# Differential attention: the second half of head 1's Q is projected during head 1 in place of head 0

## The chip, the cores and the metric

The kernel runs on one core of a Trainium2 chip. The metric is the device time of one execution in microseconds. The kernel before was timed in three runs.

## What is computed

The program is a decoder trunk of two layers over 1024 tokens of width 1024. In each layer a retention group and a differential attention group read the same normed input, their outputs are projected together, and a SwiGLU block follows. The change is in the differential attention, whose four heads each have two score matrices:

```python
dq.reshape(B, S, DIFF_HEADS, 2, DIFF_HEAD_DIM)
...
for i in range(S // Q_BLOCK):
    q0 = i * Q_BLOCK
    kend = q0 + Q_BLOCK
    ...
    s = jnp.einsum('bqhjd,bkhjd->bhjqk', qb, kb).astype(jnp.float32) * scale
    s = s - slopes[None, :, None, None, None] * dist
    s = jnp.where(dist >= 0, s, -jnp.inf)
    p = jax.nn.softmax(s, axis=-1)
    a = p[:, :, 0] - lam * p[:, :, 1]
    outs.append(jnp.einsum('bhqk,bkhe->bqhe', a.astype(vb.dtype), vb))
```

There are 8 query blocks of 128 tokens. Block i needs Q of its own 128 tokens and K and V of all tokens up to its end, so blocks 0 to 3 need only the first half (512 tokens) of Q, K and V.

## The kernel before

**Products in three parts.** An operand is kept as a high part rounded to the matmul's input type and the low part that is left, and each fp32 product is made as three matmuls (high·high, high·low, low·high; lines 288 to 290 by `mm3`). `fm_half` projects one half of the tokens for one head's Q or K: 8 blocks of the width by 3 matmuls of 128x512, so 24 matmuls into one accumulation bank `ps_mm`. `stack` then turns that bank into the two tiles that the scores read (one for each score matrix j): an ACT copy of 64x512 (line 522) and a DVE subtraction of the same size (line 523), twice. `stacks` does this for the halves that it is given, and `qk_head` for both halves of K and then both halves of Q of a head.

**One attention block** (`att_block`). The scores of block i for j=1 are made in chunks of at most 512 keys, each chunk two matmuls (lines 574 and 575) into one score bank `ps_s`. DVE adds the bias and takes the maximum of a chunk (line 577), which frees the bank; ACT takes the exponential (581) and scales by the row sum (657); then the same for j=0; the two are combined on DVE (line 666). The combined block is transposed on PE in the next block's turn (line 600), copied in two parts by ACT and DVE (605, 606), and every second block an output product follows (lines 619 to 622 into `ps_o`), with ACT's copy and square (624, 629), a split of the square in two parts (ACT line 370, DVE line 372), and the norm of each 512 tokens, whose two ones-matmuls on PE (line 380) read that split.

**Banks.** There are two score banks `ps_s`, three `ps_mm`, two `ps_t` and one `ps_o`. A chunk of scores may begin once DVE has taken the chunk that stood two before it.

**The order of the work.** PE's order is the order in which the program is written, and a scheduler sets that of ACT, DVE, POOL and SP; what stands under `high_priority` is brought forward there. `weave` (line 342) mixes an attention stretch ("main") with projections for later ("fill"): after each yield of the main stretch, which names a cost, it draws groups of three fill matmuls until the fill's share of its total has caught up with the main's share of its total. `PART0` is 72, the cost of blocks 0 to 3, and `PART1` is 92, that of blocks 4 to 7. Fill drawn within a head makes K and Q of the next head: beside blocks 4 to 7 of head 0 it is `qk_head` for head 1 (96 matmuls over 92), beside all eight blocks of head 1 it is `qk_head` for head 2 (96 over 164). Where the fill runs over, the rest is written behind the stretch.

**Transfers.** A weight is loaded by SP as one DMA of 512 KB, cast by ACT (line 280) and its low part made by POOL (line 281). `att_swap` issues four SP copies of 128 KB for a half of a head: they place K of one score matrix on the partitions on which the other's Q stands (tile `kb`).

Both layers run the same order of instructions in the attention.

Of the kernel before, what the change touches and what calls it, by code (L numbers as in the profile page):

```python
# [38 lines left out]
PART0 = HEAD + 2 * 6 + 4 * sum(LAG)  # L39
PART1 = 2 * 22 + 4 * sum(LAG)  # L40
# [107 lines left out]
class Trunk:  # L148
# [538 lines left out]
    def attention(self, l, us, w_first, norm1):  # L687
        wk, wq, wdv = w_first
        nc = self.nc
        v, qk, outs = {}, self.qk_tiles(), []  # L690
        kq = lambda hf: self.chain(self.stacks(wk, us, (hf,), qk[1], 1.0), self.stacks(wq, us, (hf,), qk[0], 0.125))
        first = [self.chain(kq(hf), self.values(wdv, us, hf, v)) for hf in range(NH)]
        if l == 0:
            for ps, st, scale in zip(self.first_ps, (qk[1], qk[0]), (1.0, 0.125)):
                f = self.tmp()
                nc.vector.tensor_tensor(out=f, in0=ps, in1=self.first_y, op=ALU.mult)
                self.stack(f, st, slice(0, HT), scale)
            self.weave(norm1, 40, self.values(wdv, us, 0, v), 48)
            self.late_consts()
        else:  # L700
            self.weave(norm1, 96, first[0], 96)
        self.prev, self.norms, self.outs = None, [], []
        for h in range(4):
            o = self.big("mx")
            outs.append(o)
            A = self.att_open(h, qk, v, o)
            nqk = self.qk_tiles() if h < 3 else None
            self.att_swap(A, 0)
            if h:
                self.att_swap(A, 1)  # L710
            if h == 0:
                self.weave(self.att_part(l, A, 0, 4), PART0, first[1], 96)
                self.att_swap(A, 1)
            elif h == 2:
                self.weave(self.att_part(l, A, 0, 4), PART0, self.values(wdv, us, 1, v), 48)
            if h == 3:
                rq = [self.big("ka") for _ in range(2)]
                rk = [self.big("a4") for _ in range(2)]
                fill = self.chain(self.ret_proj(us, rq[0], 1.0), self.ret_proj(us, rq[1], 1.0),
                                  self.ret_proj(us, rk[0], 0.125), self.ret_proj(us, rk[1], 0.125))  # L720
            else:
                fill = self.qk_head(us, nqk)
            if h % 2:
                self.weave(self.att_part(l, A, 0, 8), PART0 + PART1, fill, 96 if h == 1 else 192)
            else:
                self.weave(self.att_part(l, A, 4, 8), PART1, fill, 96)
            if h < 3:
                qk = nqk
            if h == 1:
                wdv = [self.weight(), self.weight()]  # L730
                v = {}
                self.weave(self.att_close(l), 48, self.values(wdv, us, 0, v), 48)
        return outs, rq, rk
# [556 lines left out]
```

## Time and profile before

| | us |
|---|---|
| median of three runs | 2291.52 (2290.36 to 2292.31) |
| the profiled execution | 2289.39 |
| its span in the profile | 2287.6 |
| TensorE matmul busy (share of the span) | 2251.1 (98%) |
| VectorE busy | 1404.7 (61%) |
| ScalarE busy | 1009.1 (44%) |
| GpSimd busy | 731.7 (32%) |

PE is TensorE's matmuls and PEld its weight loads, DVE is VectorE, ACT is ScalarE, POOL is GpSimd and SP is the engine that issues the DMAs. A timeline row has an instruction's start, its length, the engine, the line and the operation with output and inputs, and in square brackets the idle time before it and who ended it. Matmuls overlap: a 128x512 matmul has a length of 0.39 us on its row, and the next one starts about 0.23 us after it, so stretches of PE are reckoned from start to start. The mean granted clock was 0.996 of full speed.

### The profile page before, as it was taken

The page shows a single profiled execution, that of the slowest core. Times are in us where ns is not written, and L with a number is a line of the kernel's source. Part 1 is how long each engine was busy: PE and PEld are TensorE (multiplying, and loading weights), DVE is VectorE, ACT ScalarE, POOL GpSimd, SP SyncE. Part 2 cuts the span into 40 slices and gives each one's busy share as a digit, 9 for nine tenths or more (in the row PEclk, how much of TensorE's full clock was granted, in tenths as well). Part 3 has the DMA queues.
Part 4 walks back from the last instruction along what each step waited for, and adds up shares of the span by engine and source line. Part 5 has one row for each costly group of instructions (what it writes and reads, how often), then busy time and mean ns, then how long its engine had stood idle before and what let it go on. Part 6 is the DMA issues. An engine that isn't in the chain of part 4 may idle for free.

```text
span 2287.6 us, 30632 instructions
## 1 busy us (share of the span) xinstructions
PE 2251.1 (98%) x11328; PEld 1895.3 (83%) x11328; DVE 1404.7 (61%) x2596; ACT 1009.1 (44%) x1905; POOL 731.7 (32%) x588
## 2 busy tenths in 40 slices
PE   7999999999999999999999999999999999999998
PEld 5888898787888888888888888988878888888887
DVE  8777612989534333995567774059884434359856
ACT  5666523445333333543256665234453333344332
POOL 3111212120455555335121112211215445544350
PEclk9999999999999999999999999999999999999999
DMA  4212121112433333652232222112123232346422
GB/s 164 79 47 65 44 95 38 55 57 63 137 106 103 105 106 90 230 186 96 72 99 56 56 65 88 52 37 74 49 95 120 93 115 93 110 148 202 157 65 74
DMA packets 74215, 216.58 MB, mean 95 GB/s; under 512 B 8017, under 2 KB 10065, under 8 KB 74065
## 3 DMA queue, kind: packets, MB, share of 16 engines
q1 hardware_dynamic: 74064, 214.62, 29.1%
q8 instruction: 89, 1.46, 0.3%
q14 instruction: 62, 0.50, 0.1%
HBM read 162.16 MB, written 44.04 MB: 90 GB/s over the span
## 4 chain that ended last, share of the span: by engine, by line
PE 84%; DVE 11%; ACT 2%; issue 1%; DMA 1%; POOL 0%; SPq 0%; DVEq 0%; ACTq 0%; POOLq 0%
PE ps_mm L264 8%; PE ps_mm L265 8%; PE ps_mm L266 8%; PE ps_mm L289 7%; PE ps_mm L288 7%; PE ps_mm L290 7%; PE ps_s L265 4%; PE ps_s L264 4%; PE ps_s L266 4%; PE ps_mm L323 3%; PE ps_mm L324 3%; PE ps_mm L325 3%; PE ps_t L265 2%; PE ps_t L264 2%; PE ps_t L266 2%
## 5 line engine op out<-in xcount | busy, mean ns | idle before, releaser
L241 POOL TENSOR_TENSOR w<-wr,w 128x512 fp32r<-128x512 f32 x262 | 368.2, 1419 | 442.9 <-ACT w L240 425.6
L281 POOL TENSOR_TENSOR w<-wr,w 128x512 fp32r<-128x512 f32 x140 | 186.2, 1337 | 577.3 <-ACT w L280 520.7
L288 PE MATMUL ps_mm<-u,w 128*128 128x512 f32 (+1 forms) x735 | 296.1, 403 | 0.0
L289 PE MATMUL ps_mm<-u,w 128*128 128x512 f32 (+1 forms) x735 | 287.2, 391 | 2.4 <-DVE u L450 2.4
L290 PE MATMUL ps_mm<-u,w 128*128 128x512 f32 (+1 forms) x735 | 286.5, 390 | 0.0
L240 ACT CAST w<-wr 128x512 fp32r<-128x512 f32 x312 | 187.2, 619 | 136.5 <-DVE wr L911 77.5
L264 PE MATMUL ps_mm<-u,w 128*128 128x512 f32 x432 | 168.5, 390 | 0.0
L266 PE MATMUL ps_mm<-u,w 128*128 128x512 f32 x432 | 168.1, 389 | 0.0
L265 PE MATMUL ps_mm<-u,w 128*128 128x512 f32 x432 | 168.1, 389 | 0.0
L290 PEld LDWEIGHTS ps_mm<-u,w 128*128 128x128 f32 x735 | 138.1, 188 | 30.1
L289 PEld LDWEIGHTS ps_mm<-u,w 128*128 128x128 f32 x735 | 138.6, 189 | 26.0 <-DVE u L450 3.1
L288 PEld LDWEIGHTS ps_mm<-u,w 128*128 128x128 f32 x735 | 138.3, 188 | 23.7
L960 ACT COPY t<-ps_mm 128x512 f32<-128x512 f32 x76 | 44.7, 588 | 240.3 <-PE ps_mm L266 240.3
L280 ACT CAST w<-wr 128x512 fp32r<-128x512 f32 x140 | 85.7, 619 | 128.6 <-PE ps_t L289 39.6
L325 PE MATMUL ps_mm<-w,u 128*128 128x256 f32 x448 | 127.2, 284 | 0.8 <-DVE u L450 0.8
L323 PE MATMUL ps_mm<-w,u 128*128 128x256 f32 x448 | 128.0, 286 | 0.0
L324 PE MATMUL ps_mm<-w,u 128*128 128x256 f32 x448 | 126.9, 283 | 0.0
L241 POOL TENSOR_TENSOR w<-t,w 128x512 fp32r<-128x512 f32 x48 | 65.1, 1357 | 191.9 <-ACT w L240 191.9
L577 DVE CUSTOM_DVE_ANT_0 sp<-ps_s,wr 128x512 f32<-128x512 f32 (+2 forms) x192 | 102.9, 552 | 32.3 <-PE ps_s L575 31.3
L581 ACT ACTIVATE sp<-sp,m 128x256 f32<-128x256 f32 (+7 forms) x128 | 99.2, 775 | 50.2 <-DVE m L580 49.4
L869 DVE TENSOR_TENSOR a<-a,ps_mm 128x512 f32<-128x512 f32 (+1 forms) x148 | 98.6, 667 | 27.6 <-PE ps_mm L266 14.5
L909 DVE TENSOR_TENSOR t<-wr,wr 128x512 f32<-128x512 f32 x46 | 32.8, 712 | 119.2 <-DMA wr<-wts 118.5
(386 smaller groups left out, 5919.7 us busy)
## 6 DMA issues: line engine op xcount, KB each, us to landing
wr<-wts SPq DMA_DIRECT2D x190, 512.0 KB, 3.7
mx<-s_fast SPq DMA_DIRECT2D x56, 512.0 KB, 4.9
s_fast<-mx SPq DMA_DIRECT2D x48, 512.0 KB, 4.8
kb<-ka SPq DMA_DIRECT2D x64, 128.0 KB, 2.3
s_rest<-mx SPq DMA_DIRECT2D x12, 512.0 KB, 2.9
kb<-wts SPq DMA_DIRECT2D x12, 512.0 KB, 5.4
mx<-s_rest SPq DMA_DIRECT2D x12, 512.0 KB, 3.3
a<-xT SPq DMA_DIRECT2D x16, 256.0 KB, 5.4
```

Of the source, the lines that this page charges most:

```text
L240: nc.scalar.copy(h, src)
L241: (eng or nc.gpsimd).tensor_tensor(out=o, in0=src, in1=h.bitcast(F32), op=ALU.subtract)
L264: mm(ps, lhsT=wh[:, c], rhs=bh, start=first and i == 0, stop=False, skip_group_check=True)
L265: mm(ps, lhsT=wh[:, c], rhs=bl, start=False, stop=False, skip_group_check=True)
L266: mm(ps, lhsT=wl[:, c], rhs=bh, start=False, stop=i == 3, skip_group_check=True)
L281: nc.gpsimd.tensor_tensor(out=o, in0=raw[:, cols], in1=h.bitcast(F32), op=ALU.subtract)
L288: mm(out, lhsT=lh, rhs=rh, start=first, stop=False)
L289: mm(out, lhsT=lh, rhs=rl, start=False, stop=False)
L290: mm(out, lhsT=ll, rhs=rh, start=False, stop=last)
L323: mm(o, lhsT=uh, rhs=wh, start=k == 0, stop=False)
L324: mm(o, lhsT=uh, rhs=wl, start=False, stop=False)
L325: mm(o, lhsT=ul, rhs=wh, start=False, stop=k == KT - 1)
```

## The change

In head 0's second stretch the fill now makes K of head 1 for the first half of the tokens, Q for the first half, and K for the second half: 72 matmuls over `PART1`. Head 1's weights for K and Q are both requested ahead of it. In head 1 the fill begins with Q of head 1 for the second half of the tokens, and `qk_head` of head 2 follows: 120 matmuls over 164. Heads 2 and 3 stay as they are. In each of the two layers this moves 24 matmuls of 128x512 and one `stack`.

```diff
@@ -718,12 +718,18 @@
+            elif h == 0:
+                wk1, wq1 = self.weight(), self.weight()
+                fill = self.chain(self.stacks(wk1, us, (0,), nqk[1], 1.0), self.stacks(wq1, us, (0,), nqk[0], 0.125),
+                                  self.stacks(wk1, us, (1,), nqk[1], 1.0))
             else:
                 fill = self.qk_head(us, nqk)
+                if h == 1:
+                    fill = self.chain(self.stacks(wq1, us, (1,), qk[0], 0.125), fill)
             if h % 2:
-                self.weave(self.att_part(l, A, 0, 8), PART0 + PART1, fill, 96 if h == 1 else 192)
+                self.weave(self.att_part(l, A, 0, 8), PART0 + PART1, fill, 120 if h == 1 else 192)
             else:
-                self.weave(self.att_part(l, A, 4, 8), PART1, fill, 96)
+                self.weave(self.att_part(l, A, 4, 8), PART1, fill, 96 if h else 72)
```

**PE, the scores of block 4 of head 1 in layer 0.** The first two `ps_s` are the two chunks of block 4 for j=1, the last one is the first chunk for j=0, and `ps_mm` is the bank of a fill product. Before:

```order
L574 MATMUL ps_s_1376<-ka_472,a_106_470 128x512
L575 MATMUL ps_s_1376<-kb_1123,a_106_470 128x512
L574 MATMUL ps_s_1380<-ka_472,a_106_470 128x256
L575 MATMUL ps_s_1380<-kb_1123,a_106_470 128x256
L288 MATMUL ps_mm_1295<-u_350,w_1144 128x512
L289 MATMUL ps_mm_1295<-u_351,w_1144 128x512
L290 MATMUL ps_mm_1295<-u_350,w_1145 128x512
L574 MATMUL ps_s_1393<-ka_471,a_105_469 128x512
```

The changed kernel, the same scores:

```order
L574 MATMUL ps_s_1361<-ka_472,a_106_470 128x512
L575 MATMUL ps_s_1361<-kb_1094,a_106_470 128x512
L574 MATMUL ps_s_1365<-ka_472,a_106_470 128x256
L575 MATMUL ps_s_1365<-kb_1094,a_106_470 128x256
L288 MATMUL ps_mm_1339<-u_350,w_1227 128x512
L289 MATMUL ps_mm_1339<-u_351,w_1227 128x512
L290 MATMUL ps_mm_1339<-u_350,w_1228 128x512
L288 MATMUL ps_mm_1339<-u_350,w_1227 128x512
L289 MATMUL ps_mm_1339<-u_351,w_1227 128x512
L290 MATMUL ps_mm_1339<-u_350,w_1228 128x512
L574 MATMUL ps_s_1381<-ka_471,a_105_469 128x512
```

Two groups of three fill matmuls stand between the two score matrices where one stood. From head 0's last output product to the second of these chunks there were 30 fill matmuls and are now 33, and from it to the second j=1 chunk of block 5 there were 9 and are now 15. The other 15 of the 24 that are moved are drawn in the rest of head 1 and ahead of that product.

**ACT, behind head 0's last output product (`ps_o_1209` before, `ps_o_1176` now).** `ps_mm_1109` is the bank of head 1's Q for the second half of the tokens. Before:

```order
L624 COPY mx_464<-ps_o_1209 128x256
L629 ACTIVATE t_247_1235<-mx_464 128x512
L370 CAST t_248_1237<-t_247_1235 128x512
L581 ACTIVATE sp_1199,z_1200<-sp_1199,m_1246 128x256
L605 CAST a_252_1257<-ps_t_1261 128x128
L522 ACTIVATE ka_1128<-ps_mm_1148 64x512
```

The changed kernel:

```order
L624 COPY mx_464<-ps_o_1176 128x256
L629 ACTIVATE t_241_1202<-mx_464 128x512
L280 CAST w_1680<-wr_1674 128x512
L522 ACTIVATE a_105_469<-ps_mm_1109 64x512
L370 CAST t_242_1204<-t_241_1202 128x512
L605 CAST a_252_1239<-ps_t_1243 128x128
L581 ACTIVATE sp_1163,z_1164<-sp_1163,m_1210 128x256
L522 ACTIVATE a_106_470<-ps_mm_1109 64x512
```

A weight's cast (line 280) and the first copy of the moved `stack` (line 522) have come between the square (line 629) and its split (line 370); the second copy stands four rows on.

**DVE, around the scores of blocks 3 and 4 of head 1.** Line 577 takes a chunk of scores and frees its bank. Before:

```order
L577 ISA sp_1321,m_1344<-ps_s_1345,wr_1124 128x512
L577 ISA m_1344 128x1
L666 SCALAR_TENSOR_TENSOR sp_1269<-sp_1269,z_1270 128x384
L388 SCALAR_TENSOR_TENSOR t_261_1284<-t_260_1282,t_261_1284 128x512
L582 RECIPROCAL z_1322<-z_1322 128x1
L580 TENSOR_REDUCE m_1344<-m_1344 128x1
L636 SCALAR_TENSOR_TENSOR mx_464<-mx_464,c_dg,t_261_1284 128x512
L606 TENSOR_TENSOR a_274_1359<-ps_t_1362,a_273_1358 128x3x128
L656 TENSOR_TENSOR z_1322<-z_1322,c_nlam 128x1
L582 RECIPROCAL z_1322<-z_1322 128x1
L577 ISA sp_1373,m_1375<-ps_s_1376,wr_1124 128x512
```

The changed kernel:

```order
L666 SCALAR_TENSOR_TENSOR sp_1251<-sp_1251,z_1252 128x384
L388 SCALAR_TENSOR_TENSOR t_261_1266<-t_260_1264,t_261_1266 128x512
L582 RECIPROCAL z_1302<-z_1302 128x1
L523 SCALAR_TENSOR_TENSOR ka_1099<-ps_mm_1235,ka_1099 64x512
L636 SCALAR_TENSOR_TENSOR mx_464<-mx_464,c_dg,t_261_1266 128x512
L606 TENSOR_TENSOR a_274_1344<-ps_t_1347,a_273_1343 128x3x128
L523 SCALAR_TENSOR_TENSOR ka_1100<-ps_mm_1235,ka_1100 64x512
L656 TENSOR_TENSOR z_1302<-z_1302,c_nlam 128x1
L577 ISA sp_1301,m_1324<-ps_s_1325,wr_1095 128x512
L577 ISA m_1324 128x1
L577 ISA sp_1358,m_1360<-ps_s_1361,wr_1095 128x512
L577 ISA m_1360 128x1
```

The L577 that takes block 3's j=0 scores (`ps_s_1345`, now `ps_s_1325`) stood ahead of line 666 and now stands behind it, behind both L523 of the next `stack`, and directly ahead of the two chunks of block 4.

## Rows read from the trace of the kernel before

**Rows 1.** The page, busy time of each engine (share of the span) and instructions.

```profile
PE 2251.1 (98%) x11328; PEld 1895.3 (83%) x11328; DVE 1404.7 (61%) x2596; ACT 1009.1 (44%) x1905; POOL 731.7 (32%) x588
```

**Rows 2.** Windows: length, busy PE, PEld, DVE, ACT, POOL; clock, DMA share, GB/s.

```profile
73.50:110.30 36.80, 36.80 (x194) 31.35 (x192) 28.06 (x78) 24.96 (x46) 7.36 (x10) 1.00 0.27 72
110.30:154.80 44.50, 42.56 (x237) 35.10 (x235) 38.43 (x121) 32.07 (x70) 5.99 (x11) 1.00 0.17 44
1236.10:1280.60 44.50, 42.59 (x237) 35.09 (x236) 38.38 (x121) 32.07 (x70) 6.03 (x12) 1.00 0.17 43
```

**Rows 3.** Timeline of PE, end of head 0 and head 1's blocks 3 to 5.

```profile
104.07 0.39 PE L288 MATMUL ps_mm<-u,w 128*128 128x512 f32 x1
...
106.80 0.93 PE L600 MATMUL ps_t<-c_ident,sp 128*128 128x128 f32 x7
...
116.25 0.40 PE L288 MATMUL ps_mm<-u,w 128*128 128x512 f32 x1
...
126.28 0.39 PE L290 MATMUL ps_mm<-u,w 128*128 128x512 f32 x1
127.40 0.52 PE L600 MATMUL ps_t<-c_ident,sp 128*128 128x128 f32 x3 [0.72 <-DVE sp L666]
...
128.91 0.28 PE L574 MATMUL ps_s<-ka,a 128*128 128x256 f32 x1
...
129.62 0.39 PE L290 MATMUL ps_mm<-u,w 128*128 128x512 f32 x1
129.99 0.50 PE L574 MATMUL ps_s<-ka,a 128*128 128x512 f32 x1
...
132.87 0.39 PE L575 MATMUL ps_s<-kb,a 128*128 128x512 f32 x1
134.18 0.35 PE L574 MATMUL ps_s<-ka,a 128*128 128x256 f32 x1 [0.92 <-DVE z L656]
```

**Rows 4.** Timeline of ACT, behind head 0's last output product and at a stack.

```profile
117.19 0.63 ACT L629 ACTIVATE t<-mx 128x512 f32<-128x512 f32 x1
117.86 0.62 ACT L370 CAST t<-t 128x512 fp32r<-128x512 f32 x1
...
130.05 0.59 ACT L522 ACTIVATE ka<-ps_mm 64x512 fp32r<-64x512 f32 x1
130.54 0.61 ACT L280 CAST w<-wr 128x512 fp32r<-128x512 f32 x1
```

**Rows 5.** Timeline of DVE, head 1's blocks 1 to 3.

```profile
118.51 0.69 DVE L372 TENSOR_TENSOR t<-t,t 128x512 fp32r<-128x512 f32 x1 [0.50 <-ACT t L370]
...
119.89 0.68 DVE L523 SCALAR_TENSOR_TENSOR ka<-ps_mm,ka 64x512 fp32r<-64x512 f32 x1
120.60 0.56 DVE L577 CUSTOM_DVE_ANT_0 sp<-ps_s,wr 128x384 f32<-128x384 f32 x1
...
129.03 0.14 DVE L656 TENSOR_TENSOR z<-z,c_nlam 128x1 f32<-128x1 f32 x1
```

**Rows 6.** Timeline of DVE and PE, head 0's blocks 5 and 6.

```profile
95.95 0.56 DVE L577 CUSTOM_DVE_ANT_0 sp<-ps_s,wr 128x384 f32<-128x384 f32 x1
...
97.81 0.39 PE L574 MATMUL ps_s<-ka,a 128*128 128x512 f32 x1
...
101.01 1.15 DVE L666 SCALAR_TENSOR_TENSOR sp<-sp,z,sp 128x896 f32<-128x896 f32 x1
```

**Rows 7.** Windows around stretches in which PE did little (columns as in rows 2).

```profile
12.90:15.00 2.10, 0.93 (x9) 0.93 (x9) 2.00 (x3) 1.74 (x4) 1.33 (x1) 1.00 1.05 389
16.40:19.70 3.30, 3.30 (x5) 1.29 (x4) 2.62 (x7) 1.96 (x5) 0.89 (x2) 0.50 1.04 403
30.10:36.70 6.60, 4.50 (x19) 4.21 (x20) 6.57 (x11) 3.78 (x7) 3.05 (x3) 0.50 0.43 145
1152.60:1154.10 1.50, 0.06 (x1) 0.06 (x1) 1.50 (x3) 0.63 (x1) 0.84 (x1) 1.00 0.82 330
```

**Rows 8.** DMA issues from 60 to 160 us: KB each, us to landing.

```profile
kb<-ka SPq DMA_DIRECT2D x16, 128.0 KB, 2.4
```

## The prediction

> **What bounds the kernel now.** I read the busy times on the page first: PE's matmuls are busy for 98% of the span, DVE for 61%, ACT for 44% [rows 1]. So only two things can change the time: how much PE has to do, and where it stands still. The windows over the two stretches come next. In head 0's blocks 4 to 7 PE is busy for all of 36.80 us and DVE for 28.06 of them (76%); in head 1 PE is busy for 42.56 of 44.50 us, DVE for 38.43 (86%), and layer 1's head 1 repeats it to 0.03 us [rows 2]. PE's stops thus lie in head 1, on the side to which the change moves work. Then PE's timeline: from line 288 at 104.07 to line 600 at 106.80 stand 12 fill matmuls, so one costs 2.73 / 12 = 0.2275 us from start to start. Against that measure PE loses in head 1 126.28 to 127.40 less 0.23 = 0.89 us (transposes wait for the combined block of line 666), 132.87 to 134.18 less 0.23 = 1.08 us (a second chunk of scores waits until DVE frees a score bank) [rows 3], and some 1.4 us in nine small gaps, eight of 0.07 to 0.20 us (129.62 to 129.99 less 0.23 = 0.14 is one [rows 3]) and one of 0.38. That is 3.4 us per layer, 6.8 us in both (0.30% of the time). Of the 3.4, 1.5 lie ahead of the second j=1 chunk of block 4 at 128.91, and 1.9 behind it.
>
> **The change part by part.** All sums are against the profiled execution (2289.39 us, span 2287.6); it stands 2.1 us under the median of the runs, to which I add the difference at the end.
>
> *Work.* The 24 matmuls per layer are moved, none is added; the loads of weights and the `stack` are as many as before. PE's work changes by 0. What can change is the stops, in three places.
>
> *Head 0, from where work goes.* Between two steps of head 0 there are fewer fill matmuls, at most 12 fewer (2.73 us) between block 6's scores and its transposes. The cover that is lost there was 106.80 − (101.01 + 1.15) = 4.64 us between the end of line 666 [rows 6] and the transposes [rows 3], so 1.9 us stay. The score bank taken by line 577 until 95.95 + 0.56 = 96.51 is written at 97.81 [rows 6], a slack of 1.3 us, of which three fill matmuls (0.68) go. DVE also has one `stack` less there. I take 0.1 us per layer, between 0 and 0.3: walking the other steps in this way I find one with about 0.25 us left.
>
> *Head 1, the first stop.* The order shows that ACT does a weight's cast (line 280) and the first copy of the moved `stack` (line 522) between line 629 and line 370. Take head 0's last output product as ended at 116.25, as 0. Line 629 starts at 0.94 [rows 4], about 0.5 us later (the 0.49 us from 130.05 to 130.54 [rows 4]) line 280 at 1.45, line 522 at 1.95, which ends at 1.95 + 0.59 = 2.54; line 370 runs until about 3.1. On DVE line 372 stands behind the `stack`'s line 523 (2.6 to 3.3) and ends at 4.0. The norm's matmuls (line 380) wait for it, and PE is there at about 3.0: a stop of 1.0 us, where before line 372 was done in time.
>
> *Head 1, the second stop.* The L577 that frees the bank for block 4's second j=1 chunk now stands behind line 666, lines 388, 636, 606 and two L523. What DVE has to do up to there is what it did from 118.51 to 129.03 without an idle stretch, 10.52 us [rows 5], and the moved `stack`'s two L523, 119.89 to 120.60 each, 1.42 us [rows 5]: 11.94 us. It starts at 2.6, and waits for ACT in between; in the row of before line 372 waits 0.50 for line 370 [rows 5], and I take 0.35, between 0 and 1.0. So the bank is free at 2.6 + 11.94 + 0.35 = 14.9. PE was there at 128.91 − 116.25 = 12.66 [rows 3], less the 1.5 of stops that this holds, plus three more fill matmuls (0.68): 11.9. It loses 3.0 us, between 2.7 and 3.7, of which 1.0 at line 380 and 2.0 at this chunk. SP's queue: the four kb copies of head 1's first half are issued a few matmuls earlier than before, and land in 2.4 us [rows 8].
>
> *Head 1, behind it.* DVE had line 577 of block 4's j=0 scores behind line 606 of block 3 and has it now right behind the chunk ahead of it, and between block 4's second chunk and block 5's there are 15 fill matmuls where there were 9, 1.4 us more cover against the stop of 1.08. I take 0.2 us for what is left of the 1.9, between 0 and 0.5.
>
> *Sum per layer.* 0.1 + 3.0 + 0.2 = 3.3 us of stops against 3.4: −0.1, between 0 + 2.7 + 0 − 3.4 = −0.7 and 0.3 + 3.7 + 0.5 − 3.4 = +1.1. In both layers −0.2, between −1.4 and +2.2. The span would be 2287.4, and against the median the time is 2291.52 − 0.2 = **2291.3 us**, between 2290.1 and 2293.7. Of 0.2% (4.6 us), about what a measurement of this kernel can tell from no change, this is a twentieth.
>
> *The clock.* The new second stop is one of 2 us where the longest of before in head 1 was 1.08. Rows show both outcomes: PE was busy for 0.06 of 1.50 us at 1152.60 and the granted clock stayed 1.00; it was busy for 0.93 of 2.10 us at 12.90 and later ran a stretch of 3.30 us at 0.50, the lower of its two levels, 1.2 GHz [rows 7]. I take no fall, since head 1 shows 1.00 throughout with its own stops [rows 2], and keep the falls as rivals.
>
> The Trainium skill ("TensorE: Matmul & The Clock Gate", section "A second HAM failure mode: psum-queue depth-cycling") tells of a kernel that cycled through PSUM banks, whose TensorE idled briefly between groups so often that the clock gate swung between its levels and the cost of coming back was paid each time. Head 1 is such a place, with two score banks and eleven gaps, and its clock of 1.00 disagrees so far [rows 2]. By that rule the sum would be +6.4 in place of −0.2.
>
> **Rivals.**
>
> *Slower: the clock falls behind the 2 us stop.* Place: the second j=1 chunk of block 4, in each layer. For it speaks the stretch after 12.90, against it the one at 1152.60 [rows 7]. It decides if the stop, with the one of 1.0 us some 9 us before it, is enough for the lower level. A fall as long as the 3.30 us row costs half, 1.65 us: +1.4 to +3.1 in all for one layer or both, still within 0.2% (2293.0 to 2294.6). A fall as long as the 6.60 us row at 30.10 [rows 7] costs 3.3 us in each layer: −0.2 + 6.6 = +6.4, **2297.9**. One long fall alone equals two short ones.
>
> *Faster: the stops go.* If what counts is the share of DVE, and not the order in which the scheduler puts it, the change evens it out: head 1 gets 24 × 0.2275 = 5.46 us of matmuls but only 1.4 us of DVE work, (38.43 + 1.4) / (44.50 + 5.46) = 80% in place of 86%, and head 0 (28.06 − 1.4) / (36.80 − 5.46) = 85%, up from 76% [rows 2]. For it: a fuller PE stream covers each wait of head 1 by 6 to 12 matmuls more in the later blocks. Against it: both new stops hang on one place early in the head, where DVE runs without idle and only three fill matmuls are added. All of the stops gone gives −6.8, **2284.7**; it passes 0.2% from 4.6 of the 6.8 on, when less than 1.1 us per layer is left, that is, when the second stop doesn't come.
>
> *Slower: SP's queue.* Three of the four copies of K's second half for head 1 now stand behind a weight's load that waits for a slot POOL has to free. They have about 12 us until block 4. If the load is held longer than that, PE waits for at least one landing, 2.4 us [rows 8], in each layer, or for two, one behind the other: −0.2 + 4.8 = +4.6 to −0.2 + 9.6 = +9.4, **2296.1 to 2300.9**. Against it: POOL is busy for 5.99 of 44.50 us here [rows 2].
>
> **How the numbers follow.** Forecast (stops change place, total within −1.4 to +2.2) 0.57; short falls of the clock 0.18; faster 0.12; long falls in both layers 0.10; SP's queue 0.03. Faster by over 0.2%: 0.12. Within: 0.57 + 0.18 = 0.75. Slower: 0.10 + 0.03 = 0.13. The range takes in the forecast, the short falls and the long ones up to 2298.0. At the lower end it reaches from 2290.1 to 2288.5, since the walk over some thirty instructions of DVE, which fixes 3.0, may be off by another 0.8 per layer. It leaves out the faster case and the queue, 0.15. The forecast's own range is 2288.5 to 2293.7.
>
> **What would show it.** Right: in each layer PE waits about 1 us at line 380 (ones-matmul into `ps_o`) and about 2 us at the second j=1 chunk of head 1's block 4, for a chunk of line 577; the stops of 0.89 and 1.08 us are gone, or under 0.3; head 0 has no stop over 0.3; the clock is 1.00 in both stretches; PE's busy time is the same. Wrong: a granted clock of 0.50 behind block 4 (the clock); no wait at that chunk (the faster rival, or DVE's walk); a wait of block 4's scores on a kb copy (SP's queue); a stop over 0.3 us in head 0's blocks 6 and 7 (the cover there).

## The result and the profile after

The changed kernel takes 2296.95 us (median of 11 runs), the kernel before 2290.55 (11 runs, those shown among them): a ratio of 1.0028 with a 95% interval of 1.0021 to 1.0036, so 6.4 us slower. One of the eleven executions took 3210.22 us at a mean granted clock of 0.65 and stands outside the interval; without it the median is 2296.93. The forecast was 2291.3 us and no change to be told, with a range of 2288.5 to 2298.0. The measured time lies in the range, but on the side (slower by over 0.2%) that had a chance of 0.13.

The profiled execution of the changed kernel took 2295.90 us. The page's busy times:

```profile
span 2294.1 us, 30644 instructions
PE 2252.5 (98%) x11328; PEld 1896.2 (83%) x11328; DVE 1409.2 (61%) x2596; ACT 1008.5 (44%) x1905; POOL 728.6 (32%) x588
```

Against [rows 1] PE has the same instructions and 1.4 us more busy time, while the span has grown by 6.5 us. The place is found by windows over head 0's second stretch and head 1 together, up to the end of head 1's fill. The window of the kernel before (columns as in [rows 2]):

```profile
73.40:154.76 81.36, 79.42 (x429) 66.51 (x428) 66.55 (x199) 56.99 (x115) 13.45 (x21) 1.00 0.22 56
```

The same window of the changed kernel:

```profile
73.40:158.00 84.60, 79.85 (x429) 66.82 (x428) 70.07 (x200) 57.09 (x115) 13.04 (x21) 1.00 0.22 55
```

The two heads take 3.2 us more in layer 0; in layer 1, by the first value matmul behind head 1, it is 3.2 us too (84.52 in place of 81.34 us), and nothing else in the program differs by as much as that. PE's clock is 1.00. Two numbers are to be seen. PE stands still for 84.60 − 79.85 = 4.75 us where it stood for 1.94. And DVE is busy for 70.07 us in place of 66.55, 3.5 us more, **with the same work**: some of its instructions take longer.

PE's waits in that stretch, of the changed kernel (us in total, times, longest):

```profile
PE ps_s L574 <- DVE m L577: 3.2, 2, 2.2
PE ps_o L619 <- ACT a L605: 0.8, 1, 0.8
PE ps_o L380 <- DVE t L372: 0.4, 1, 0.4
PE ps_o L379 <- ACT t L370: 0.2, 1, 0.2
```

Its timeline of PE at these waits, where [rows 3] showed 127.40 and 134.18:

```profile
115.17 0.34 PE L575 MATMUL ps_s<-kb,a 128*128 128x384 f32 x1
115.76 0.51 PE L379 MATMUL ps_o<-t,c_ones 128*128 128x512 f32 x1 [0.25 <-ACT t L370]
116.69 0.50 PE L380 MATMUL ps_o<-t,c_ones 128*128 128x512 f32 x1 [0.43 <-DVE t L372]
...
125.35 0.40 PE L575 MATMUL ps_s<-kb,a 128*128 128x512 f32 x1
127.95 0.39 PE L574 MATMUL ps_s<-ka,a 128*128 128x256 f32 x1 [2.21 <-DVE m L577]
...
133.47 0.28 PE L575 MATMUL ps_s<-kb,a 128*128 128x256 f32 x1
134.54 0.39 PE L619 MATMUL ps_o<-a,v 128*128 128x256 f32 x1 [0.79 <-ACT a L605]
...
141.17 0.39 PE L575 MATMUL ps_s<-kb,a 128*128 128x512 f32 x1
142.54 0.44 PE L574 MATMUL ps_s<-ka,a 128*128 128x384 f32 x1 [0.98 <-DVE m L577]
```

From start to start, less one matmul of its size, PE loses 0.42 + 0.70 = 1.12 us at the norm's matmuls and 2.37 at block 4's second chunk: the two stops that were forecast. The two behind them, 0.95 at the output product of blocks 2 and 3 and 1.14 at block 6's second j=1 chunk (128x384; the expectation of the scalar form below names it by block 5's second j=0 chunk, whose bank it waits for), were not. Both begin on DVE, at line 656, which multiplies one factor per row by lambda (128x1):

```profile
101.06 0.84 DVE L656 TENSOR_TENSOR z<-z,c_nlam 128x1 f32<-128x1 f32 x1
...
131.00 1.14 DVE L656 TENSOR_TENSOR z<-z,c_nlam 128x1 f32<-128x1 f32 x1
132.06 0.28 DVE L577 CUSTOM_DVE_ANT_0 sp<-ps_s,wr 128x128 f32<-128x128 f32 x1
...
140.82 1.20 DVE L656 TENSOR_TENSOR z<-z,c_nlam 128x1 f32<-128x1 f32 x1
142.05 0.42 DVE L577 CUSTOM_DVE_ANT_0 sp<-ps_s,wr 128x256 f32<-128x256 f32 x1
...
156.37 1.05 DVE L656 TENSOR_TENSOR z<-z,c_nlam 128x1 f32<-128x1 f32 x1
```

The 12 of these instructions in the same stretch of the kernel before took 0.145 to 0.160 us, as their group's row shows (minimum, median and maximum in ns):

```profile
L656 DVE TENSOR_TENSOR z<-z,c_nlam x12: 145/155/160, 77.8 to 154.2; 128x1 f32<-128x1 f32 x12
```

In the changed kernel the 12 take 5.5 us together, where they took 1.9: that is where DVE's 3.5 us come from. The last long one, at 156.37, costs PE nothing: no wait of PE stands behind it.

On POOL, line 281 (the low part of a weight) runs in the changed kernel at just those times:

```profile
100.61 1.29 POOL L281 TENSOR_TENSOR w<-wr,w 128x512 fp32r<-128x512 f32 x1 [4.38 <-DVE z L582]
...
130.83 1.30 POOL L281 TENSOR_TENSOR w<-wr,w 128x512 fp32r<-128x512 f32 x1 [14.76 <-ACT w L280]
140.72 1.29 POOL L281 TENSOR_TENSOR w<-wr,w 128x512 fp32r<-128x512 f32 x1 [8.60 <-ACT w L280]
```

They end at 101.90, 132.13 and 142.01, and the three lines 656 at 101.90, 132.14 and 142.02. In the second case ACT's scaling, exponential and copy of the transposes (lines 657, 581 and 605) follow late and the output product waits; in the third, line 577 behind it frees its bank late. This is the theory that the runs had to test: **POOL's line 281 holds DVE's line 656.** The rivals: DVE simply has too much to do in head 1; or the order that the new fill share gives ACT and DVE makes the stops.

The Trainium skill ("SBUF — State Buffer", section "SBUF: two separate sides") has a rule for it: VectorE and GpSimd share a pair of SBUF ports, and of a GpSimd instruction that reads SBUF and a VectorE instruction with two inputs in SBUF, the one that starts first keeps the pair to its end while the other waits. The three pairs of ends above agree.

### The profile page after: what moved, and what is told of

The parts are those of the page before. It is cut to its first block, busy times and chain, and to the rows that moved or that the text cites. A ratio compares the mean times of both kernels' runs of the same rounds, so it can differ in the third digit from the quotient of the medians.

```text
span 2294.1 us, 30644 instructions
## 1 busy us (share of the span) xinstructions
PE 2252.5 (98%) x11328; PEld 1896.2 (83%) x11328; DVE 1409.2 (61%) x2596; ACT 1008.5 (44%) x1905; POOL 728.6 (32%) x588
## 4 chain that ended last, share of the span: by engine, by line
PE 86%; DVE 10%; ACT 2%; issue 1%; DMA 1%; POOL 0%; SPq 0%; DVEq 0%; ACTq 0%; POOLq 0%
PE ps_mm L264 8%; PE ps_mm L265 8%; PE ps_mm L266 8%; PE ps_mm L288 7%; PE ps_mm L289 7%; PE ps_mm L290 7%; PE ps_s L265 4%; PE ps_s L264 4%; PE ps_s L266 4%; PE ps_mm L324 3%; PE ps_mm L323 3%; PE ps_mm L325 3%; PE ps_t L264 3%; PE ps_t L266 3%; PE ps_t L265 3%; PE ps_s L574 1%
## 5 line engine op out<-in xcount | busy, mean ns | idle before, releaser
L577 DVE CUSTOM_DVE_ANT_0 sp<-ps_s,wr 128x512 f32<-128x512 f32 (+2 forms) x192 | 102.8, 552 | 27.8 <-PE ps_s L575 27.0
```

## The experiments

**Line 656 away from DVE.**

```diff
-        nc.vector.tensor_tensor(out=z[:, 3:4], in0=z[:, 3:4], in1=self.nlam[:, l:l + 1], op=ALU.mult)
+        nc.scalar.mul(z[:, 3:4], z[:, 3:4], self.nlam[:, l:l + 1])
```

> The changed kernel, with the multiplication of the row factor by lambda (line 656, 128x1) on ACT in place of DVE; PE's and POOL's order stay the same. Theory (POOL holds DVE): in the changed kernel's trace line 656 takes 1.14 and 1.20 us in place of 0.15 while POOL's line 281 runs, and the two waits of PE behind it (0.79 at line 619 and 0.98 at line 574 in head 1, in each layer) come from that. They should fall under 0.2, and the time by 3 to 4.2 us, from +6.4 to about +2.5 us against the kernel before. Rival (DVE's own work in head 1): both waits stay within 0.2 us, and the time within 1 us of the changed kernel.

(In what follows, "over" and "under" are against the runs of the kernel before on the same chip, whose medians were 2289.92, 2290.29 and 2289.36 us.)

Measured: 2289.91 us, a ratio to the kernel before of 0.9999 (0.999 to 1.0008). All of the 6.4 us is gone, more than the 4.2 expected. PE's waits in the two heads of layer 0:

```profile
PE ps_s L574 <- DVE m L577: 1.6, 3, 0.7
PE ps_o L380 <- DVE t L372: 0.4, 1, 0.4
```

The wait at line 619 is gone; but the 2.2 us at block 4 are down to 0.7 as well, since DVE's order changed with the edit. So this run speaks for the theory without settling it.

**Line 656 in its place on DVE, with one SBUF tensor in place of two.**

```diff
-        nc.vector.tensor_tensor(out=z[:, 3:4], in0=z[:, 3:4], in1=self.nlam[:, l:l + 1], op=ALU.mult)
+        nc.vector.tensor_scalar(out=z[:, 3:4], in0=z[:, 3:4], scalar1=self.nlam[:, l:l + 1], scalar2=None, op0=ALU.mult)
```

> The changed kernel with line 656 still on DVE and in the same places (PE's and POOL's order the same, DVE's in head 1 up to block 6 the same), but written as a tensor_scalar (the factor as a per-partition scalar) in place of a tensor_tensor with two SBUF tensors. Theory (it is the second SBUF tensor that makes DVE wait for POOL's line 281, which reads two SBUF tensors): the longest line 656 falls from 1.20 to under 0.3 us, the waits at line 619 (0.8) and at block 5's second j=0 chunk (1.0) fall under 0.3 each, the second stop (2.2 at block 4) stays, and the time falls by 3 to 4.5 us against the changed kernel, to +2 to +3.5 against the kernel before. Rival (any DVE instruction on SBUF is held, or line 656 waits for its operand): line 656 stays at 1 us or more and the time within 1 us of the changed kernel.

Measured: 2291.71 us, ratio 1.0008 (0.9999 to 1.0017): 1.4 us over the kernel before in place of 6.4, and the two heads take 82.2 us per layer in place of 84.6. The group of line 656 in this run (minimum, median and maximum in ns):

```profile
L656 DVE TENSOR_SCALAR z<-z,c_nlam x64: 206/214/217, 54.8 to 1406.2; 128x1 f32<-128x1 f32 x64
```

PE's waits in the two heads of layer 0:

```profile
PE ps_s L574 <- DVE m L577: 2.3, 1, 2.3
PE ps_o L380 <- DVE t L372: 0.4, 1, 0.4
PE ps_o L379 <- ACT t L370: 0.2, 1, 0.2
```

Two of the instructions, on DVE's timeline:

```profile
129.91 0.21 DVE L656 TENSOR_SCALAR z<-z,c_nlam 128x1 f32<-128x1 f32 x1
138.81 0.21 DVE L656 TENSOR_SCALAR z<-z,c_nlam 128x1 f32<-128x1 f32 x1
```

And POOL's beside them:

```profile
129.74 1.29 POOL L281 TENSOR_TENSOR w<-wr,w 128x512 fp32r<-128x512 f32 x1 [14.78 <-ACT w L280]
138.71 1.29 POOL L281 TENSOR_TENSOR w<-wr,w 128x512 fp32r<-128x512 f32 x1 [7.67 <-ACT w L280]
```

Line 656 still falls into line 281 and takes 0.21 us. In head 1 the order of PE, ACT, DVE and POOL is the changed kernel's up to block 6. Just the two unforeseen waits are gone, and the two that were forecast stand as they were. This settles it for 2.4 of the 3.2 us per layer. The fall is 5.0 us, over the 4.5 expected, since head 0's hold at 101.06, and the losses of 0.17 and 0.24 us behind it, went as well. (There ACT's and DVE's orders changed too; that these losses are the hold's is shown by the halves below.)

The whole traces say the same. Of the 64 lines 656 of the kernel before, 8 began with over 0.2 us of a line 281 still to run, and of the changed kernel's 16: each of these 24 ended within 0.02 us of that line 281. In the scalar form 18 began so, and none took over 0.22 us. Nor was line 577 held, which reads a score bank in place of a second SBUF tensor: of its 128x512 form 12 began so in the kernel before, and none took longer by over 0.01 us.

The control, the kernel before with the same edit:

> The kernel before with the same tensor_scalar for line 656: a control. In its trace no line 656 of head 0 or 1 fell on a line 281 of POOL. Theory: the time is within 1 us of the kernel before. Rival (the edit makes every block cheaper, whatever POOL does): 2 us or more faster than the kernel before.

Measured: 2290.91 us, 0.6 us over, ratio 1.0001 (0.9992 to 1.001). The edit by itself brings nothing. In the two heads of the kernel before no line 656 fell into a line 281; the eight that did stand elsewhere, and took 0.25 to 1.06 us. They went with the edit and the time did not fall, so as far as this run tells (ACT's and DVE's orders changed with it) they cost nothing: a hold costs time only where PE waits behind it.

**Line 281 in two halves**, with the order of PE, DVE and ACT as in the changed kernel, row by row.

```diff
-            nc.gpsimd.tensor_tensor(out=o, in0=raw[:, cols], in1=h.bitcast(F32), op=ALU.subtract)
+            for c in range(2):
+                q = slice(256 * c, 256 * c + 256)
+                r = slice(512 * i + 256 * c, 512 * i + 256 * c + 256)
+                nc.gpsimd.tensor_tensor(out=o[:, q], in0=raw[:, r], in1=h[:, q].bitcast(F32), op=ALU.subtract)
```

> The changed kernel, with POOL's low part of a weight (line 281, 128x512, 1.3 us) made as two instructions of 128x256. Theory (POOL holds DVE): an instruction of DVE can be held for one POOL instruction at most, so the longest line 656 falls from 1.20 to about 0.7 us, the two waits of PE behind it lose about 0.5 us each, and the time falls by some 2 us. Rival (DVE's own work): line 656 stays at 1.1 to 1.2 us where it was, and the time within 1 us.

Measured: 2291.49 us, 1.6 us over in place of 6.4, ratio 1.001 (1.0001 to 1.0019). Line 656 (659 with the added lines) takes 0.72 us at the longest:

```profile
L659 DVE TENSOR_TENSOR z<-z,c_nlam x64: 151/159/717, 56.7 to 1410.7; 128x1 f32<-128x1 f32 x64
```

The dose works: half of the POOL instruction, a hold half as long. The wait at line 619 went, that at block 6's second j=1 chunk fell from 0.98 to 0.42. In head 0 line 656 takes 0.30 in place of 0.84, and the losses of 0.17 and 0.24 us are gone. But the two heads got only 0.3 us shorter in layer 0 of this profile, because here the granted clock did fall to the lower of its levels (0.50, 1.2 GHz) behind the stop of block 4, as it did in layer 1. The windows of the stop and of what follows it:

```profile
126.20:128.80 2.60, 0.40 (x2) 0.00 (x0) 2.51 (x7) 1.05 (x2) 0.00 (x0) 1.00 0.00 0
128.80:132.40 3.60, 3.60 (x10) 2.91 (x11) 2.07 (x9) 2.28 (x6) 0.07 (x1) 0.53 0.00 0
```

For a stretch after 2.6 us in which PE was busy for 0.40, the matmuls stood 0.43 us apart; from the late chunk to the second chunk of j=0 it took 3.75 us (128.80 to 132.55) where the changed kernel took 2.18 (127.95 to 130.13), so the fall cost about 1.6. So part of the gain of this kernel lies elsewhere in the program (the last two runs, below). This execution took 2294.05 us, the longest of that kernel's eleven, which went down to 2290.29. The profile of the changed kernel shows no such fall, and its execution of 2295.90 us was the fastest of its own. That some of the others, up to 2298.3, had one is likely and not shown.

**The fill's share of head 1 back at 96**, with the move kept.

```diff
-                self.weave(self.att_part(l, A, 0, 8), PART0 + PART1, fill, 120 if h == 1 else 192)
+                self.weave(self.att_part(l, A, 0, 8), PART0 + PART1, fill, 96 if h == 1 else 192)
```

> The changed kernel with one number back: the fill's total in head 1 is 96 again in place of 120, the moved Q half and its place ahead of head 2's K stay. 24 fill matmuls are then written behind head 1's blocks. The order puts line 370 ahead of line 522 on ACT again, and on DVE line 577 of block 3's j=0 scores ahead of line 666, as before. Theory (the order of DVE and ACT, which the share sets, makes the stops, not the amount of work that is moved): the waits at lines 379 and 380 (0.68 us together) and at block 4's second chunk (2.2 us) are under 0.3 each, and the time is within 2 us of the kernel before. Rival (the added DVE work in head 1 makes them): the waits in head 1 still sum to over 3 us per layer, and the time is 4 us or more over the kernel before.

Measured: 2292.35 us, 2.4 us over, ratio 1.001 (1.0002 to 1.0019): nearer to the theory's 2 us than to the rival's 4. The waits at 379, 380 and block 4's second j=1 chunk are gone, as the order said. PE's waits in the two heads of layer 0 are now:

```profile
PE ps_t L600 <- DVE sp L666: 1.0, 2, 0.7
PE ps_s L574 <- DVE z L656: 0.9, 1, 0.9
PE ps_s L574 <- DVE m L577: 0.6, 1, 0.6
```

Their sum, 2.5 us, lies between the 1.8 of the kernel before and the 4.6 of the changed one. So the two stops that were forecast hang on the share, by the order that it leads to, and not on the move alone. (The share also changes how much DVE has to do in the first blocks; the two were not told apart.)

With the scalar form of line 656 as well:

> The changed kernel with the fill's total of head 1 at 96 and line 656 as a tensor_scalar. In the run with 96 alone a line 656 of head 0 took 0.84 us under a line 281 and the transposes behind it waited 0.68 us. Theory: that wait goes, and the time falls by 1 to 1.6 us against 96 alone, to about +1 us against the kernel before, or no difference from it. Rival (the waits of 96 alone come from elsewhere): no change within 0.5 us.

Measured: 2291.17 us, 0.9 us over, ratio 1.0003 (0.9994 to 1.0012). That is 1.5 us less than without it, as expected of a hold of 0.84 us per layer that is taken away. (ACT's and DVE's orders in head 0 changed with the edit too.)

**The move undone, head 0's new order kept.**

```diff
-                                  self.stacks(wk1, us, (1,), nqk[1], 1.0))
+                                  self.stacks(wk1, us, (1,), nqk[1], 1.0), self.stacks(wq1, us, (1,), nqk[0], 0.125))
...
-                if h == 1:
-                    fill = self.chain(self.stacks(wq1, us, (1,), qk[0], 0.125), fill)
```

> The changed kernel with the move undone: Q's second half is made in head 0 again, as its last fill, with totals of 96; what stays is the order of head 0's fill (K first half, Q first half, K second half, Q second half) and both weights requested ahead. Theory (the move and its share cost all of it): within 1.5 us of the kernel before. Rival (the new order of fill and weight loads in head 0 costs something): the waits or the short losses in head 0 stay as in the changed kernel, and the time is 2 us or more over the kernel before.

Measured: 2293.53 us, ratio 1.0017 (1.0008 to 1.0026). The rival was right here: the new order of head 0's fill, with both weights requested ahead, costs 3.6 us without any move. A wait of 0.90 us at line 619 has come to head 1's start. Ahead of it, in head 0, POOL holds line 387 (1.54 us for 128x512) and line 666 (1.89 for 128x896). To see whether that is the cause, line 281 was halved here too:

> The kernel with the move undone (head 0's fill in the new order K, Q, K, Q, 3.6 us over the kernel before), with POOL's line 281 in two halves; the order of PE, DVE and ACT is the same, row by row. In the trace of the undone kernel POOL held two DVE instructions of head 0, line 387 (1.54 us for 128x512 where it takes 0.69) and line 666 (1.89 for 128x896 where it takes 1.15). Theory (what the new order of head 0 costs is the hold too): these two lose about half of their excess, PE's wait of 0.90 at line 619 behind them falls to 0.5 or less, and head 0 with head 1 gets shorter by 0.4 us or more per layer. Rival (the wait at line 619 comes from ACT's own order there, two line 522 and two line 581 ahead of line 605): it stays at 0.8 to 1.0 us.

Measured: 2293.32 us, 4.0 us over, ratio 1.0019 (1.001 to 1.0028). Both holds got shorter (line 387 1.00 us, line 666 1.33 or less), but the wait at line 619 rose to 1.26 us and one of 1.84 at a transpose came. Neither the theory nor the rival expected that. ACT shows where it begins, at a weight's cast that stands ahead of block 7's row scaling:

```profile
108.10 0.62 ACT L280 CAST w<-wr 128x512 fp32r<-128x512 f32 x1 [3.50 <-PE ps_mm L293]
```

The weight's load landed 0.10 us ahead of it, 5.4 us after its issue; the same load took 3.7 us in the undone kernel, where this cast waited 0.23. Why it took longer was not looked into. In the undone kernel's timeline of ACT the copy that PE waits for stands behind a second line 522 and two exponentials of head 1:

```profile
113.36 0.59 ACT L522 ACTIVATE a<-ps_mm 64x512 fp32r<-64x512 f32 x1 [1.34 <-DVE a L523]
113.98 0.40 ACT L581 ACTIVATE sp<-sp,m 128x128 f32<-128x128 f32 x1
...
114.38 0.38 ACT L581 ACTIVATE sp<-sp,m 128x128 f32<-128x128 f32 x1
...
114.89 0.58 ACT L605 CAST a<-ps_t 128x512 fp32r<-128x512 f32 x1
```

So this run does not tell what the hold costs in this order, since a later load came with the halves. That ACT's order makes the wait of 0.90 is read from these rows and was not tried. What the 3.6 us are stays open.

**The bank freed first**: the scalar form of line 656, and line 577 under priority.

```diff
+            with self.tc.high_priority():
                 nc.vector.tensor_tensor_reduce(
```

> The kernel of the tensor_scalar edit, and line 577, which frees a score bank, given priority over other DVE work, so that the one for block 3's j=0 scores stands ahead of both L523 and of lines 388, 636 and 606. Theory (the second stop is an order of DVE, not its load): the wait of 2.2 us at block 4's second j=1 chunk falls under 0.5, and the time falls by 2 to 4 us against the tensor_scalar edit alone. Rival (DVE has too much to do in head 1, the stop moves on): PE's waits in head 1 sum to as much as there, within 0.7 us per layer, since what stood behind (lines 666 and 606) is late next.

Measured: 2298.23 us, 7.9 us over, ratio 1.0034 (1.0021 to 1.0046), where the scalar form alone was 1.4 over. The stop moved, as the rival said; its row on PE's timeline:

```profile
131.47 0.33 PE L601 MATMUL ps_t<-c_ident,sp 128*128 128x128 f32 x1 [2.33 <-DVE sp L667]
```

Line 666 (667 here) is late in place of 577. Behind the moved stop the granted clock fell to its lower level in this profile too, in both layers; the window in layer 0:

```profile
132.80:136.30 3.50, 3.50 (x17) 3.31 (x16) 2.60 (x7) 0.80 (x2) 0.00 (x0) 0.52 0.00 0
```

The priority also holds for all other blocks: heads 2 and 3 take 1.3 us more per layer than with the scalar form alone. So the 7.9 us are not the price of the moved stop alone. Putting this one line first does not take the stop away. That DVE's order has no part in it is not shown: with line 656 on ACT the order is another one, and 0.7 of the 2.2 us were left there.

**Line 281 in halves, in the two fastest versions.**

> The kernel before with line 281 in two halves, the order of PE, DVE and ACT the same. Its trace has one such hold in head 1, line 666 with 0.98 us for 128x384 where the changed kernel has 0.61, and the transposes wait for it. Theory: that line gets shorter by 0.1 to 0.4 us, and the time changes by 0 to −1 us in the attention; in the changed kernel's run with halves the stretch from head 3 to layer 1 was some 2 us shorter than in other runs, and if that is the halves' doing, the time falls by 2 to 3 us here. Rival (that stretch varies from run to run): within 1 us of the kernel before.

Measured: 2286.47 us, 2.9 us under, ratio 0.999 (0.9981 to 0.9999). The hold of line 666 that was to get shorter did not (1.12 us in place of 0.98), and the two heads stayed at 81.5 us. The gain is elsewhere. Among the waits of the whole run of the kernel before stand these two:

```profile
PE ps_mm L289 <- DVE u L450: 2.4, 2, 1.5
PE ps_o L835 <- DVE mx L793: 2.2, 4, 1.0
```

In the run with halves they are, three lines on:

```profile
PE ps_o L838 <- DVE mx L796: 1.1, 4, 0.4
PE ps_mm L292 <- DVE u L453: 0.4, 1, 0.4
```

They are in the retention and where a layer's first projections wait for the normed input. Other waits of the run rose and fell by up to 0.7 us. Why the halves help was not looked into further.

> The changed kernel with line 656 on ACT, which was level with the kernel before (ratio 0.9999), and line 281 in two halves as well. There line 636 of head 0 took 1.39 us (0.75 elsewhere) under a line 281, and PE's wait of 0.68 behind it. Theory: that wait falls by 0.3 us or more per layer, and the time to 1 to 3 us under the kernel before, the fastest of the versions. Rival: no change within 0.5 us, since the longer waits there are DVE's order.

Measured: 2286.74 us, 2.6 us under, ratio 0.9989 (0.998 to 0.9998). The time is the theory's, its way there is not: line 636 (639 here) fell from 1.39 to 0.83 us, but the wait of 0.68 behind it stayed at 0.68, and the gain is again outside the two heads. Both versions with halves beat both kernels by a little, and can't be told from each other.

## Why the prediction was wrong

**The bound, and the work.** Right. PE bounds the kernel, its instructions are as many, and the time went into its stops.

**Head 0.** The term was 0.1 us per layer, with an upper end of 0.3. Block 6's transposes, for which a cover of 1.9 us was worked out, lost nothing: line 666 ended at 99.86 and they began at 101.29. Two new losses at block 7, 0.17 us ahead of its transposes and 0.24 ahead of the output product, make 0.4. The walk through these other steps took line 656 at its usual length. At 101.06 it took 0.84, and with the 0.30 of the halves both losses are gone.

**First and second stop.** Right in place and mechanism, and 0.5 us short in size: 1.12 + 2.37 = 3.5 in place of 3.0, within the bounds of 2.7 to 3.7. The experiments bear it out at both: with the share back at 96 they are gone; with line 577 ahead the wait moves to line 666.

**Behind it: this step failed.** "I take 0.2 us for what is left of the 1.9, between 0 and 0.5." There were 0.95 + 1.14 = 2.1 us. The old stops of 0.89 and 1.08 are gone as the cover argument said (124.09 and 133.36 begin without a wait); two new ones came. The argument counted DVE's order and the cover of fill matmuls, and took each DVE instruction at its length in the trace of before. The change also moved POOL's line 281, with the weights' casts on ACT, onto line 656, and there a 0.15 us instruction takes 1.14 and 1.20. The prediction names POOL only as a queue that SP waits for. It did not ask what POOL's instructions do to DVE's, although the trace of before shows it. In the stretch of [rows 5] a line 666 (0.98 us for 128x384, 0.61 in the changed kernel) was held in just this way, under a line 281 from 125.42 to 126.84, and in other heads line 656 itself took up to 1.06 us (POOL's row, DVE's row, and line 656's group over the whole trace):

```profile
125.42 1.42 POOL L281 TENSOR_TENSOR w<-wr,w 128x512 fp32r<-128x512 f32 x1 [8.74 <-ACT w L280]
...
126.27 0.98 DVE L666 SCALAR_TENSOR_TENSOR sp<-sp,z 128x384 f32<-128x384 f32 x1
...
L656 DVE TENSOR_TENSOR z<-z,c_nlam x64: 144/159/1058, 55.4 to 1405.5; 128x1 f32<-128x1 f32 x64
```

The 0.89 us that the transposes lost behind that line 666 are one of the two stops from which the prediction starts.

**The sum.** By the measured terms it is 0.4 + 3.5 + 2.1 = 6.0, and some 0.5 in gaps of about 0.1: 6.5 us per layer against 3.4, +3.1. In both layers that is +6.2, where 6.4 were measured and −0.2 was forecast. Of the 3.2 us per layer between this and the forecast of −0.1, 1.9 are the failed term, 0.5 the size of the two stops, 0.3 head 0 and the rest small gaps. The one edit that takes the hold away gives back 2.4 us per layer, the failed term and head 0's.

**The rivals.** The clock: it names the difference that was measured, +6.4, by a cause that was not at work in the profiled execution. That one is 6.5 us longer at a clock of 1.00 throughout the two heads. The mechanism exists, as the profiles of the halves and of line 577 first show, and such falls may account for the spread above 2295.9. SP's queue: no wait on a kb copy is to be seen in head 1. The stops going with the evened shares: no; DVE's share over both heads even rose, 70.07 of 84.60 us in place of 66.55 of 81.36.

## What to carry to other kernels

When a change moves work on PE, look where it moves the *other* engines' instructions against each other, POOL's long ones above all, and check each DVE instruction with two SBUF tensors that may fall on them: a tiny one on the path costs what is left of the POOL instruction, and one off the path costs nothing (that at 156.37). In a trace of before, the same shape with two lengths is the sign (0.16 and 1.06 us of line 656 here), and an engine that is busy for longer with the same instructions is the sign after. The remedies are cheap: one SBUF tensor and a per-partition scalar, another engine, or shorter POOL instructions; the halves came with a later load in one order here.

## What the runs showed of the hardware

- POOL's tensor_tensor of 128x512 from SBUF (1.29 us) held DVE's tensor_tensor of 128x1 up to its own end (1.14 and 1.20 us in place of 0.15); as a tensor_scalar with a per-partition factor it ran inside the same POOL instruction in 0.21 us. With POOL's instruction in halves the longest line 656 was 0.72 us.
- A stop of PE of 2.2 to 2.3 us at the same chunk, with the same matmuls ahead of it and behind it, was followed by a granted clock of 1.00 in two profiles (the changed kernel and its scalar form) and of 0.53, a mean with the lower level of 1.2 GHz in it, in another (the halves).
